# Feed-forward stages of a hybrid decoder trunk on one core: VectorE's order written out in gate and up, block sums placed tile by tile, and residual halves loaded ahead in down

## The chip, the cores and the metric

The kernel runs on one core of a Trainium2 chip. The metric is the device time of one execution in microseconds (us), as the median of several runs; less is better. The engines are TensorE (PE in the profile, PEld for its weight loads), VectorE (DVE), ScalarE (ACT), GpSimd (POOL) and SyncE (SP), which here does nothing but issue transfers (DMAs). Each engine takes its instructions in its own order and waits at an instruction until what it needs is there.

## The reference

Two layers on x of 1 x 1024 x 1024, float32. Each layer is a mix of windowed attention and a gated convolution, and then the feed-forward part, where most of this change lies:

```
h = rmsnorm(x, norm_mix); one projection h @ w_in -> q | k | v | conv value | conv gate | gate_A | gate_B
A = sliding-window attention (16 heads of 64, 2 KV heads, q and k normed, partial rotary, sinks)
B = GLU -> causal depthwise conv (width 31) -> LayerNorm -> swish -> pointwise projection
x = x + (sigmoid(gate_A) * A + sigmoid(gate_B) * B) @ w_out
h = rmsnorm(x, norm_ffn)
x = x + (silu(h @ w_gate) * (h @ w_up)) @ w_down          # D_FF = 2816 = 22 tiles of 128
```

## The kernel before, in words

All activations lie transposed: channels on partitions, the 1024 tokens along the free axis. A product of float32 matrices is made of three matmuls on parts, hi x hi, hi x lo and lo x hi. A weight is loaded raw (`fraw`, `wraw`), ACT casts its high part (`phi`, L149), and POOL or DVE subtracts that from it for the low part (`plo`, L151). `piece` does this for 512 columns. The generator `stream` yields the pieces of one layer's feed-forward in the order in which TensorE uses them; `next_p` hands out the next and keeps `PAHEAD` = 6 of them made ahead, in `NPC` = 8 buffers for each part, from 3 raw buffers.

**Gate and up.** The 22 tiles of D_FF come in the order `FORD`: 0, 11, 1, 12, and so on, so that tile p and tile p + 11 follow each other. The first two (`NCL`) are plain products. The other 20 are done as 2 x 2 block products with 7 multiplications in place of 8 (a Strassen form): gate and up are the two rows of the weight block, the two halves of the tokens the columns. Each of the 7 is 4 x 3 matmuls of 128 x 512 into a PSUM bank: `b1`, `b6`, `b7`, `b5`, `b4`, and then the products "21" and "22", which accumulate further into `b1` and `b5`. Between them DVE reads the banks: `u2` (L973), `u3` (L977), the second half of u from `b5` (L980), the first half from `b4` (L983), u times the norm factor R (L984), g's first half (L986) and second half (L988, L989). "22" can only start once L980 has read `b5`. The weight side needs sums as well: four of 512 columns for each tile (`fs`, L164).

`finish` then does silu on g (ACT, L918), g x u (POOL, L919) and the store of act (SP, L920). After the second tile of two, p + 11, it also makes the four differences of the two tiles' g that the down stage needs (DVE, L926), and stores them as `td`. Two of them overwrite the g whose store to act is under way, so they wait for it to land.

The down weights need four sums of 512 columns for each of the 11 pairs of row tiles (`dw`, L164), with two loads (L191, L192) and two stores to `sd` (L197, L198). They stand inside `stream`, so they are put into the program when the pieces ahead of them are asked for.

**Down.** Seven products again (`DOWN`: p1, p6, p2, p7, p5, p4, p3), each of 11 steps p; a step has one piece of weights and one of activations (both from memory: `wdn` or `sd`, `act` or `td`) and 4 x 3 matmuls into four banks, 132 matmuls in all. The products alternate between two sets of four banks. The last three steps (`FL` = 3) are taken together, bank by bank, so that the banks end one after the other. `evict` then reads a bank, for p2, p5, p4 and p3 into a half of the residual that `half_of` loads (L1014) at that moment (for p3 ahead of the last three steps, with `us` added, L1072); `done` writes it out and, in layer 0, makes layer 1's input from it.

**Order.** TensorE's instructions stay in the order in which the program issues them (a manual schedule). DVE's do too in a part of the in-projection; elsewhere a scheduler sets the order of DVE, ACT, POOL and SP by its own model of the times. `after(n, fn)` calls fn n ticks later; `tick()` is called at set places, as after each step of the projections, and `flush()` runs what is left.

## Time and profile before

| | us |
|---|---|
| median of 3 runs | 2760.35 (2757.0 to 2761.77) |
| the profiled execution | 2754.2 |
| its span, first to last instruction | 2752.4 |
| mean granted clock of TensorE | 0.974 |

The profile is of one execution. Durations and waits below are of that one, which is 6.15 us shorter than the median. The page's slices show three kinds of stretches: a projection, attention and convolution stretch with TensorE at 80 to 100%, then gate and up (the Strassen tiles from 756 us in layer 0 and 2121 us in layer 1) and down (1166 to 1389 us, 2534 to 2748 us). The groups of the page that belong to the feed-forward part:

```profile
L149 ACT CAST phi<-fraw 128x512 fp32r<-128x512 f32 x444 | 265.8, 620 | 500.8 <-PE b L857 344.2
L151 DVE TENSOR_TENSOR plo<-fraw,phi 128x512 fp32r<-128x512 f32 x154 | 182.4, 1191 | 143.4 <-ACT phi L149 141.4
L926 DVE TENSOR_TENSOR g<-g 128x512 f32<-128x512 f32 x88 | 119.9, 1363 | 113.2 <-DMA act<-g 63.0
```

Each line names the program line, the engine, the operation, output <- input with their shapes, the count, the busy time in us and the mean of one in ns; then the engine's idle time just before them and what ended most of it.

### The profile page before, as it was taken

The numbers are of one execution on the slowest core, as the hardware profiler recorded it, in microseconds if no ns is written. First come the engines' busy times: TensorE is split into PE (matmuls) and PEld (weight loads), VectorE is DVE, ScalarE is ACT, GpSimd is POOL, SyncE is SP. The second block draws the span as 40 slices with busy tenths as digits, with TensorE's granted clock in tenths as the row PEclk, the third lists the DMA queues.
The fourth block names the chain that finished last, engine by engine and source line by source line (L and its number), as shares of the span: only waits on it lengthen the run. The fifth ranks groups of instructions, "written<-read, shape, count | busy, mean of one in ns | idle before, by whom it ended". The sixth has DMA issues, their size and how long they took to land.

```text
span 2752.4 us, 33203 instructions
## 1 busy us (share of the span) xinstructions
PE 2596.1 (94%) x11736; PEld 2121.1 (77%) x11736; DVE 1930.6 (70%) x2053; ACT 1208.3 (44%) x2211; POOL 1598.4 (58%) x1052
## 2 busy tenths in 40 slices
PE   7998988999989999999999889899999889999998
PEld 5777777888777788878777777778887768888887
DVE  6799999551788666656737999995518777676554
ACT  2356666832522223345523666667325222323443
POOL 6477778525365666554435778775254556665544
PEclk9999999999999999999999999999999999999999
DMA  3111111475366432366721111125733654334666
GB/s 127 40 50 48 56 58 62 157 248 193 107 237 229 153 115 100 132 225 224 226 68 42 49 56 50 48 76 185 269 138 118 238 211 164 109 118 146 211 225 199
DMA packets 132358, 379.05 MB, mean 138 GB/s; under 512 B 15136, under 2 KB 15392, under 8 KB 132192
## 3 DMA queue, kind: packets, MB, share of 16 engines
q1 hardware_dynamic: 132048, 376.85, 40.1%
q8 instruction: 92, 1.51, 0.2%
q14 instruction: 74, 0.61, 0.1%
q10 hardware_dynamic: 144, 0.09, 0.0%
HBM read 259.17 MB, written 115.34 MB: 136 GB/s over the span
## 4 chain that ended last, share of the span: by engine, by line
PE 44%; DVE 15%; DMA 5%; issue 2%; ACT 2%; POOL 1%; SPq 0%; DVEq 0%; ACTq 0%; POOLq 0%
PE b L857 32%; PE ps L255 10%; DVE y L509 6%; DVE dw L164 1%; DMA dw<-wdn 1%; DVE qs L626 1%; DMA sd<-dw 1%; DVE mx L662 1%; DVE plo L151 1%; DVE sc L658 1%; ACT sc L666 1%; ACT phi L149 1%; DMA act<-g 1%; DMA fraw<-act 1%; DVE fs L164 0%
## 5 line engine op out<-in xcount | busy, mean ns | idle before, releaser
L151 POOL TENSOR_TENSOR plo<-fraw,phi 128x512 fp32r<-128x512 f32 x290 | 418.7, 1451 | 386.1 <-ACT phi L149 352.2
L149 ACT CAST phi<-fraw 128x512 fp32r<-128x512 f32 x444 | 265.8, 620 | 500.8 <-PE b L857 344.2
L509 DVE SCALAR_TENSOR_TENSOR y<-a,vec,y 128x1024 f32<-128x1024 f32 x240 | 404.8, 1687 | 4.0
L134 POOL TENSOR_TENSOR wl<-raw,wh 128x1024 fp32r<-128x1024 f32 (+1 forms) x100 | 252.0, 2522 | 230.9 <-PE ps L255 192.6
L255 PE MATMUL ps<-hx,wh 128*128 128x512 f32 x1056 | 348.8, 412 | 7.3 <-ACT hx L296 7.3
L255 PE MATMUL ps<-hx,wl 128*128 128x512 f32 x1056 | 336.3, 400 | 6.9 <-POOL wl L134 6.9
L255 PE MATMUL ps<-lx,wh 128*128 128x512 f32 x1056 | 338.2, 402 | 0.8 <-DVE lx L297 0.8
L151 POOL TENSOR_TENSOR plo<-fs,phi 128x512 fp32r<-128x512 f32 x160 | 233.2, 1473 | 117.0 <-ACT phi L149 115.0
L151 DVE TENSOR_TENSOR plo<-fraw,phi 128x512 fp32r<-128x512 f32 x154 | 182.4, 1191 | 143.4 <-ACT phi L149 141.4
L857 PE MATMUL b<-plo,phi 128*128 128x512 f32 x616 | 241.8, 393 | 10.0 <-DVE plo L151 10.0
L255 PEld LDWEIGHTS ps<-hx,wl 128*128 128x128 f32 x1056 | 204.7, 194 | 52.7 <-POOL wl L134 7.8
L255 PEld LDWEIGHTS ps<-lx,wh 128*128 128x128 f32 x1056 | 205.9, 195 | 48.4 <-DVE lx L297 2.2
L857 PE MATMUL b<-phi 128*128 128x512 f32 x616 | 240.5, 390 | 1.9 <-ACT phi L149 1.9
L857 PE MATMUL b<-phi,plo 128*128 128x512 f32 x616 | 240.5, 390 | 1.2 <-POOL plo L151 1.2
L255 PEld LDWEIGHTS ps<-hx,wh 128*128 128x128 f32 x1056 | 195.1, 197 | 42.8 <-ACT hx L296 7.3
L926 DVE TENSOR_TENSOR g<-g 128x512 f32<-128x512 f32 x88 | 119.9, 1363 | 113.2 <-DMA act<-g 63.0
L149 ACT CAST phi<-fs 128x512 fp32r<-128x512 f32 x160 | 97.7, 617 | 191.3 <-PE b L857 141.5
L919 POOL TENSOR_TENSOR g<-g,u 128x1024 f32<-128x1024 f32 x44 | 107.6, 2445 | 123.7 <-ACT g L918 84.0
L666 ACT ACTIVATE sc<-sc,nm,fq 128x129 f32<-128x129 f32 x256 | 123.7, 486 | 116.0 <-DVE nm L664 115.7
L133 ACT CAST wh<-raw 128x1024 fp32r<-128x1024 f32 (+1 forms) x100 | 98.2, 982 | 167.6 <-PE ps L255 115.8
L857 PEld LDWEIGHTS b<-plo,phi 128*128 128x128 f32 x616 | 115.9, 188 | 38.5 <-DVE plo L151 14.7
L857 PEld LDWEIGHTS b<-phi 128*128 128x128 f32 x616 | 116.0, 188 | 26.9 <-ACT phi L149 2.6
(253 smaller groups left out, 6226.0 us busy)
## 6 DMA issues: line engine op xcount, KB each, us to landing
fraw<-wgu SPq DMA_DIRECT2D x88, 512.0 KB
raw<-win SPq DMA_DIRECT2D x68, 512.0 KB
act<-g SPq DMA_DIRECT2D x44, 512.0 KB
dw<-wdn SPq DMA_DIRECT2D x44, 512.0 KB
sd<-dw SPq DMA_DIRECT2D x44, 512.0 KB
td<-g SPq DMA_DIRECT2D x44, 512.0 KB
fraw<-sd SPq DMA_DIRECT2D x88, 256.0 KB
fraw<-td SPq DMA_DIRECT2D x88, 256.0 KB
```

Source lines behind the costliest of these rows:

```text
L133: nc.scalar.copy(wh, raw)
L134: nc.gpsimd.tensor_tensor(out=wl, in0=raw, in1=wh.bitcast(F32), op=ALU.subtract)
L149: nc.scalar.copy(hi, src)
L151: (eng or nc.gpsimd).tensor_tensor(out=lo, in0=src, in1=hi.bitcast(F32), op=ALU.subtract)
L164: sub = lambda o, a, b, op=ALU.subtract: nc.vector.tensor_tensor(out=o, in0=a, in1=b, op=op)
L255: nc.tensor.matmul(ps[:, sl], a[:, wc], b[:, sl], start=first and j == 0, stop=last and j == 2)
L509: nc.vector.scalar_tensor_tensor(out=y, in0=a[:, j:j + T], scalar=V(w0 + j), in1=y, op0=ALU.mult, op1=ALU.add)
L626: after(1.5 + h, lambda hi=hi, lo=lo, h=h: nc.vector.tensor_tensor(out=qs[h][lo], in0=q32[hi], in1=qs[h][hi].bitcast(F32), op=ALU.subtract))
L666: nc.scalar.activation(sc[:, n], sc[:, n], AF.Exp, bias=nm[:, n:n + 1], scale=fq[:, 4 * j + n:4 * j + n + 1], accum_out=den[:, n:n + 1])
L857: nc.tensor.matmul(ps, w[:, ai * P:(ai + 1) * P], x, start=first and j == 0, stop=last and j == 2, skip_group_check=True)
L919: nc.gpsimd.tensor_tensor(out=g, in0=g, in1=u, op=ALU.mult)
L926: sub = lambda o, x, y: nc.vector.tensor_tensor(out=o, in0=x, in1=y, op=ALU.subtract)
```

## The change

1. **DVE's order in gate and up.** For the 20 Strassen tiles DVE gets a manual schedule as well, and the program calls `tick()` after each of the 7 products. What DVE does beside the evictions is placed by `after`.
2. **Block sums.** The sums of `dw`, their loads and stores leave `stream`. `block_sums(p, when)` makes the four of one pair at ticks 3, 4, 5, 6 of every second tile (pair 10 first, in the first Strassen tile, then pair 0, 1, and so on).
3. **finish by halves.** Silu and g x u are done for 512 columns at a time, the first half after product "21". Two of the differences of g come three ticks after the second half, the other two and the stores of `td` one tick later.
4. **Down.** Only p3 keeps its last three steps bank by bank; the others do that with the last step alone. The residual halves are loaded at steps 1 to 4 of the product that uses them (`HALVES`), and for p4 and p3 `u3` or `us` is added to them at steps 4 to 7.
5. **Buffers.** 7 piece buffers instead of 8, 5 pieces ahead instead of 6, 4 raw buffers instead of 3.
6. **Layer 1's keys and values.** The second half of K's product ends before that of V's begins; the input norm's factors are computed at once there, and the rotary step, its sum and a transpose move by one or two ticks.

```diff
-            for p in range(NG):                      # in stream()
-                if max(2 * p, NCL + 1) != i + (p == 0):
-                    continue
-                lo, up = (fq.tile([P, D], F32, tag=f"dw{k}", bufs=1, name="dw") for k in range(2))
-                nc.sync.dma_start(lo, wdn[l, p])
...
-        def finish(f, g, u):
-            nc.scalar.activation(g, g, AF.Silu)
-            nc.gpsimd.tensor_tensor(out=g, in0=g, in1=u, op=ALU.mult)
+        def finish(f, g, u, sl=slice(0, T)):
+            nc.scalar.activation(g[:, sl], g[:, sl], AF.Silu)
+            nc.gpsimd.tensor_tensor(out=g[:, sl], in0=g[:, sl], in1=u[:, sl], op=ALU.mult)
+            if sl.stop < T:
+                return
             nc.sync.dma_start(actd[f], g)
...
+            def late():
+                subs((b[:, h1], b[:, h1], a[:, h0]), (b[:, h0], b[:, h1], b[:, h0]))
+                nc.sync.dma_start(tdn[f - NG], a)
+                nc.sync.dma_start(tdn[f], b)
+            after(3, lambda: subs((a[:, h0], a[:, h1], a[:, h0]), (a[:, h1], b[:, h1], a[:, h1])))
+            after(4, late)
+
+        def block_sums(p, when):
+            lo, up = (fq.tile([P, D], F32, tag=f"dw{k}", bufs=1, name="dw") for k in range(2))
+            nc.sync.dma_start(lo, wdn[l, p])
+            nc.sync.dma_start(up, wdn[l, p + NG])
+            def last():
+                subs((up[:, h0], up[:, h0], lo[:, h0]))
+                nc.sync.dma_start(sdn[p], lo)
+                nc.sync.dma_start(sdn[p + NG], up)
+            after(when[0], lambda: nc.vector.tensor_tensor(out=up[:, h1], in0=lo[:, h1], in1=up[:, h1], op=ALU.add))
+            after(when[1], lambda: subs((lo[:, h1], lo[:, h0], lo[:, h1])))
+            after(when[2], lambda: subs((lo[:, h0], up[:, h1], lo[:, h0])))
+            after(when[3], last)
...
+        dve.enter_context(tc.manual_schedule(engines={mybir.EngineType.DVE}))
...
+            if i % 2:
+                block_sums(i // 2 - 1, (3, 4, 5, 6))
+            elif i == NCL:
+                block_sums(NG - 1, (5, 5.5, 6, 6.5))
...
             prod4(b1, next_p(), B["21"], False, True)
-            nc.vector.tensor_tensor(out=g[:, h0], in0=b1, in1=R[:, h0], op=ALU.mult)
+            add(g[:, h0], b1, R[:, h0], ALU.mult)
+            finish(f, g, u, h0)
+            tick()
...
-                x = half_of(e, 0)                    # evict, p2; p5 and p4 alike
+                x = left[e]
...
+            fl = FL if name == "p3" else 1
+            for p in range(NG - fl):
                 w, a = next_p(), next_p()
                 for e in range(4):
                     prod(bs[e], w, e, a[0], a[1], go and p == 0, False)
...
+                if 1 <= p < 5 and name in HALVES:
+                    up, n = HALVES[name]
+                    left[p - 1] = half_of(p - 1 + up, n)
+                if 4 <= p < 8 and name in ("p3", "p4"):
+                    x, u = left[p - 4], us[p - 4] if name == "p3" else u3[p - 4]
+                    nc.vector.tensor_tensor(out=x, in0=x, in1=u, op=ALU.add)
...
-        for i, (k, ns) in enumerate(kn):
-            for w, ps in ((wk, psk), (wv, psv)):
+            steps = [(k, (0, 1), both) for k in range(4, KD)] + [(k, (0,), both) for k in range(4)]
+            steps += [(k, (1,), (x,)) for x in both for k in range(4)]
...
-NPC = 8
-PAHEAD = 6
+HALVES = {"p2": (0, 0), "p5": (4, 1), "p4": (4, 0), "p3": (0, 1)}
+NPC = 7
+PAHEAD = 5
+NRAW = 4
```

What this does to the order of the engines shows in the listings below, one instruction or a run of alike ones a row. In these, `u_` with a number is u2 or u3 of a tile, `u` without one the tile's u.

DVE in gate and up of layer 0, before, in the sixth Strassen tile, one with differences of g (L926) in it:

```order
L973 TENSOR_TENSOR u_6707<-b,s 128x512
L926 TENSOR_TENSOR g<-g 128x512
L977 TENSOR_TENSOR u_6740<-b,u_6707 128x512
L926 TENSOR_TENSOR g<-g 128x512
L980 TENSOR_TENSOR u<-b,u_6740 128x512
L926 TENSOR_TENSOR g<-g 128x512
L164 TENSOR_TENSOR dw<-dw 128x512 x2
L983 TENSOR_TENSOR u<-u_6740,b 128x512
L164 TENSOR_TENSOR dw<-dw 128x512
L984 TENSOR_TENSOR u<-u,R 128x1024
```

And now, in a tile of the same kind (L978 is the helper of the evictions, L911 that of the differences):

```order
L978 TENSOR_TENSOR u_7953<-b,s 128x512
L911 TENSOR_TENSOR g<-g 128x512 x2
L164 TENSOR_TENSOR fs<-fraw,fs 128x512
L978 TENSOR_TENSOR u_7976<-b,u_7953 128x512
L911 TENSOR_TENSOR g<-g 128x512 x2
L978 TENSOR_TENSOR u<-b,u_7976 128x512
L164 TENSOR_TENSOR fs<-fraw 128x512
L164 TENSOR_TENSOR fs<-fs,fraw 128x512
L978 TENSOR_TENSOR u<-u_7976,b 128x512
L978 TENSOR_TENSOR u<-u,R 128x1024
```

The block sums have left this tile for its neighbours, and all four differences of g stand ahead of the addition into u that was L980.

SP in gate and up of layer 0, before, at the pairs 1 to 3 (`dw` loads, `sd` and `td` stores, `act` stores):

```order
L920 DMA act_1_5022<-g 128x1024
L197 DMA sd_2_5067<-dw 128x1024
L198 DMA sd_13_5078<-dw 128x1024
L191 DMA dw<-wdn 128x1024
L156 DMA fraw<-wgu 128x1024
L192 DMA dw<-wdn 128x1024
L156 DMA fraw<-wgu 128x1024
L197 DMA sd_3_5068<-dw 128x1024
L198 DMA sd_14_5079<-dw 128x1024
L191 DMA dw<-wdn 128x1024
```

And now, from the same act store's neighbours on:

```order
L928 DMA td_11_5054<-g 128x1024
L940 DMA sd_10_5075<-dw 128x1024
L941 DMA sd_21_5086<-dw 128x1024
L156 DMA fraw<-wgu 128x1024
L935 DMA dw<-wdn 128x1024
L936 DMA dw<-wdn 128x1024
L156 DMA fraw<-wgu 128x1024
L918 DMA act_1_5022<-g 128x1024
L940 DMA sd_0_5065<-dw 128x1024
L941 DMA sd_11_5076<-dw 128x1024
```

Between two act stores of a pair stood two sets of block sums' stores and loads; now pair 10's set stands ahead of them and pair 0's behind act_1, and from there on one set comes to two tiles.

DVE in layer 1's down stage, before, from the end of p4 to p3's additions of `us` to the residual half (L1072; L1035 is the eviction, `plo` the pieces' low parts):

```order
L151 TENSOR_TENSOR plo<-fraw,phi 128x512 x6
L1035 TENSOR_TENSOR x<-x,b 128x512 x3
L1072 TENSOR_TENSOR x<-x,us_20043 128x512
L151 TENSOR_TENSOR plo<-fraw,phi 128x512
L1035 TENSOR_TENSOR x<-x,b 128x512
L1072 TENSOR_TENSOR x<-x,us_20044 128x512
L151 TENSOR_TENSOR plo<-fraw,phi 128x512 x9
```

And now (L1105 adds `us`, L1066 is the eviction):

```order
L151 TENSOR_TENSOR plo<-fraw,phi 128x512 x7
L1066 TENSOR_TENSOR x<-x,b 128x512 x4
L151 TENSOR_TENSOR plo<-fraw,phi 128x512 x2
L1105 TENSOR_TENSOR x<-x,us_20122 128x512
L151 TENSOR_TENSOR plo<-fraw,phi 128x512
L1105 TENSOR_TENSOR x<-x,us_20123 128x512
L151 TENSOR_TENSOR plo<-fraw,phi 128x512 x6
```

Two of the additions of `us` stood in the midst of the evictions before; now the evictions are done together, and those two follow behind two more low parts.

More of the change, by code (lines that the diff above doesn't have):

```diff
@@ L154, in wraw @@
     def wraw(src, n=KD * P):
-        r = fw.tile([P, n], F32, tag="fraw", bufs=3, name="fraw")
+        r = fw.tile([P, n], F32, tag="fraw", bufs=NRAW, name="fraw")
         nc.sync.dma_start(r, src)
@@ L185, in stream @@
             yield piece(s4)
[L186 to L198 removed]
         for _, (a, ac), (b, bc) in DOWN:
             for p in range(NG):
[L201 removed]
+                r = fw.tile([P, D], F32, tag="fraw", bufs=NRAW, name="fraw")
                 for o, src, (row, col), w in ((c0, (wdn[l], sdn), ac, a), (c1, (actd, tdn), bc, b)):
@@ L424, in keys @@
             nc.scalar.activation(sq, ps, AF.Square)
-            rope(k32)
+            after(1 if l else NA + 0.5, lambda: rope(k32))
             f8 = sm.tile([P, 16], F32, tag="f8", name="f8")
@@ L456, in keys @@
             when_free('po', 6, norm)
-            after(7, lambda: rope_add(k32))
-            when_free('pT', 10, lambda: turn(0))
+            after(9, lambda: rope_add(k32))
+            when_free('pT', 11, lambda: turn(0))
             when_free('pT', 13, lambda: turn(1))
@@ L751, in trunk @@
         psv = psm.tile([P, 4, 2 * P], F32, tag="S", bufs=1, name="psv").rearrange("p a b -> p (a b)")
-        kn = [(k, (0, 1)) for k in range(KD)]
+        both = ((wk, psk), (wv, psv))
+        steps = [(k, (0, 1), both) for k in range(KD)]
         if l > 0:
-            kn = [(k, (0, 1)) for k in range(4, KD)] + [(k, (n,)) for n in range(2) for k in range(4)]
-        for i, (k, ns) in enumerate(kn):
-            for w, ps in ((wk, psk), (wv, psv)):
-                mm3(ps, w, slice(k * P, (k + 1) * P), xs[k], i == 0, k == kn[-1][0], ns)
-            if k < KD - 1 and (l == 0 or ns != (0,) or k % 2):
+            steps = [(k, (0, 1), both) for k in range(4, KD)] + [(k, (0,), both) for k in range(4)]
+            steps += [(k, (1,), (x,)) for x in both for k in range(4)]
+        for i, (k, ns, wps) in enumerate(steps):
+            for w, ps in wps:
+                mm3(ps, w, slice(k * P, (k + 1) * P), xs[k], i == 0, k == steps[-1][0], ns)
+            if i < 7:
                 tick()
-        after(NA, norm_a)
+        after(0 if l else NA, norm_a)
         dve = ExitStack()
@@ L915, in spread, with subs @@
                 nc.vector.tensor_tensor(out=bl, in0=t, in1=bh.bitcast(F32), op=ALU.subtract)
-        def finish(f, g, u):
-            nc.scalar.activation(g, g, AF.Silu)
-            nc.gpsimd.tensor_tensor(out=g, in0=g, in1=u, op=ALU.mult)
+        first = []
+        def subs(*ops):
+            for o, x, y in ops:
+                nc.vector.tensor_tensor(out=o, in0=x, in1=y, op=ALU.subtract)
+        def finish(f, g, u, sl=slice(0, T)):
[3 more added lines that the diff above has]
+                return
             nc.sync.dma_start(actd[f], g)
@@ L962, in half @@
             return fq.tile([P, HALF], F32, tag="c", bufs=4, name=name)
-        for f in FORD[NCL:]:
+        dve = ExitStack()
+        dve.enter_context(tc.manual_schedule(engines={mybir.EngineType.DVE}))
+        add = lambda o, x, y, op=ALU.add: nc.vector.tensor_tensor(out=o, in0=x, in1=y, op=op)
+        for i, f in enumerate(FORD):
+            if i < NCL:
+                continue
+            if i % 2:
+                block_sums(i // 2 - 1, (3, 4, 5, 6))
+            elif i == NCL:
+                block_sums(NG - 1, (5, 5.5, 6, 6.5))
             g, u = t4("g"), t4("u")
@@ L972, in trunk @@
             u2 = half("u2")
-            nc.vector.tensor_tensor(out=u2, in0=b6, in1=s, op=ALU.add)
+            add(u2, b6, s)
+            tick()
             b7 = bank()
@@ L1064, in trunk @@
             go, end = name not in ("p2", "p3"), name not in ("p1", "p5")
-            for p in range(NG - FL):
+            fl = FL if name == "p3" else 1
+            for p in range(NG - fl):
                 w, a = next_p(), next_p()
@@ L1068, in trunk @@
                     prod(bs[e], w, e, a[0], a[1], go and p == 0, False)
-            if name == "p3":
-                for e in range(4):
-                    left[e] = half_of(e, 1)
-                    nc.vector.tensor_tensor(out=left[e], in0=left[e], in1=us[e], op=ALU.add)
-            wa = [(next_p(), next_p()) for _ in range(FL)]
+                if 1 <= p < 5 and name in HALVES:
[4 more added lines that the diff above has]
+                    nc.vector.tensor_tensor(out=x, in0=x, in1=u, op=ALU.add)
+            wa = [(next_p(), next_p()) for _ in range(fl)]
             for e in range(4):
                 for i, (w, a) in enumerate(wa):
-                    prod(bs[e], w, e, a[0], a[1], False, end and i == FL - 1)
+                    prod(bs[e], w, e, a[0], a[1], False, end and i == fl - 1)
                 evict(name, e, bs[e])
```

42 lines of the change are left out of this document (16 added, 26 removed).

## The prediction

> **What bounds the kernel now.** I read the page's first part, then busy time by stretches (the two feed-forward blocks cut at their stages), then the waits of TensorE, and last the timeline around one long wait. The page first:
>
> ```profile
> PE 2596.1 (94%) x11736; PEld 2121.1 (77%) x11736; DVE 1930.6 (70%) x2053; ACT 1208.3 (44%) x2211; POOL 1598.4 (58%) x1052
> ```
>
> TensorE is busy for 94% of the span and its work is not changed, so only its gaps and its slow matmuls can be won. Which stage holds them? The next rows give, for a stretch of the span: length, busy time and instruction count of PE, PEld, DVE, ACT and POOL, granted clock, DMA share, GB/s. In order they are layer 0's first 7 Strassen tiles of gate and up and its last 13, the same for layer 1 (8 and 12), and the down stage of layer 0 and of layer 1; then three single tiles and three single down products.
>
> ```profile
> 755.90:914.90 159.00, 142.96 (x590) 114.39 (x589) 130.88 (x144) 39.66 (x64) 91.22 (x57) 0.96 0.64 232
> 914.90:1166.10 251.20, 251.20 (x1094) 205.32 (x1093) 163.17 (x182) 75.22 (x117) 152.53 (x101) 1.00 0.32 113
> 2120.90:2301.90 181.00, 164.03 (x673) 131.71 (x673) 143.85 (x156) 44.70 (x71) 105.30 (x65) 0.94 0.60 216
> 2301.90:2533.80 231.90, 231.90 (x1009) 189.53 (x1008) 158.06 (x168) 68.38 (x108) 143.98 (x93) 1.00 0.32 113
> 1166.10:1389.10 223.00, 214.23 (x925) 173.46 (x924) 140.46 (x140) 110.43 (x184) 110.28 (x76) 0.99 0.67 220
> 2533.90:2748.20 214.30, 209.98 (x925) 173.07 (x923) 116.59 (x114) 89.63 (x152) 104.36 (x74) 1.00 0.67 219
> ...
> 755.90:776.56 20.66, 19.59 (x85) 15.71 (x84) 19.92 (x22) 5.36 (x9) 15.70 (x9) 1.00 0.63 223
> 799.50:824.67 25.17, 21.94 (x85) 17.48 (x84) 19.15 (x24) 5.78 (x10) 11.91 (x8) 0.88 0.67 243
> 914.90:934.20 19.30, 19.30 (x86) 15.79 (x85) 14.18 (x18) 5.79 (x10) 11.56 (x8) 1.00 0.38 137
> 1203.34:1233.26 29.92, 29.92 (x133) 24.78 (x132) 16.24 (x15) 13.14 (x24) 15.06 (x12) 1.00 0.61 194
> 1166.09:1203.34 37.25, 32.90 (x133) 25.32 (x132) 18.35 (x15) 17.05 (x27) 20.50 (x12) 0.95 0.77 270
> 2714.95:2748.22 33.27, 30.21 (x133) 24.52 (x131) 13.96 (x16) 10.58 (x18) 13.02 (x10) 1.00 0.50 164
> ```
>
> The last 13 and 12 tiles run with PE busy throughout: 251.20 / 13 = 19.32 us a tile. That is the floor. The first 7 and 8 take 22.7 and 22.6 us each, DVE is 82% and 79% busy in them (130.88 of 159.00, 143.85 of 181.00), and the DMA share is twice that of the later tiles. The excess is 159.00 - 7 x 19.32 = 23.7 and 181.00 - 8 x 19.32 = 26.4, together 50.1 us. A down product's floor is 29.92 us; the excess there is 223.0 - 209.4 = 13.6 and 214.3 - 209.4 = 4.9, together 18.4 us. So 68.5 us is all that these two stages can give. The waits of PE for line 857 (all products) over the whole run: sum, times, longest.
>
> ```profile
> PE b L857 <- DVE u L980: 33.0, 13, 4.9
> PE b L857 <- DVE plo L151: 10.0, 10, 3.1
> PE b L857 <- POOL plo L151: 1.2, 1, 1.2
> ```
>
> L980 is the addition that reads bank b5 for the second half of u; the product "22" then accumulates into b5 and can't start before. Thirteen waits for one DVE operation make 33.0 of the 50.1. What kept it is in the timeline of the tile of 25.17 us, and of the one of 20.66:
>
> ```profile
> 773.67 0.50 PE L857 MATMUL b<-B22h,phi 128*128 128x512 f32 x1 [1.07 <-DVE u L980]
> ...
> 811.61 1.75 DVE L926 TENSOR_TENSOR g<-g 128x512 f32<-128x512 f32 x1 [1.70 <-POOL g L919]
> 811.63 0.45 SPq L920 DMA_DIRECT2D act<-g  x1
> ...
> 815.57 0.40 PE L857 MATMUL b<-B21l,phi 128*128 128x512 f32 x1
> 815.80 0.40 PE L857 MATMUL b<-B21h,plo 128*128 128x512 f32 x1
> 817.24 1.53 DVE L926 TENSOR_TENSOR g<-g 128x512 f32<-128x512 f32 x1 [3.27 <-DMA act<-g]
> 818.69 0.68 DVE L980 TENSOR_TENSOR u<-b,u 128x512 f32<-128x512 f32 x1
> 819.43 0.79 PE L857 MATMUL b<-B22h,phi 128*128 128x512 f32 x1 [3.23 <-DVE u L980]
> 820.45 0.63 PE L857 MATMUL b<-B22h,plo 128*128 128x512 f32 x1
> ```
>
> DVE stood idle for 3.27 us at a subtraction of g that may not overwrite g until the store of act, issued at 811.63, had landed; L980 stood behind it. PE waited 3.23 us, and its matmuls then begin 0.43 to 0.6 us apart instead of 0.23: the tile ran at a granted clock of 0.88 and took 5.85 us more than the floor, not 3.23. After the wait of 1.07 us the clock stayed at 1.00 and the tile took 20.66 - 19.32 = 1.34 more. So 17.1 of the 50.1 us is slow matmuls after waits.
>
> The Trainium skill, TensorE: Matmul & The Clock Gate, section "Part 1: The HAM clock gate", says that an idle window of about 3.4 us halves the array's clock and some 3.4 us of work restores it. If each of the 13 waits set it off, an estimate by that page is 13 x 1.7 = 22 us beside the 33.0, 5 more than the tiles lost, and the forecast would be 5 lower; the trace agrees in kind, but the short wait lost nothing, so I go by the tiles.
>
> **Gate and up.** DVE's work around those tiles, as groups (count, busy, mean ns, idle before); the first row from 760 to 960 us, the others but the L989 one from 960 to 1150, where there are no block sums. The L989 row, over both, gives minimum, median and maximum in ns; the L919 row is the page's, and the last, of the chain that ended last, has start and length.
>
> ```profile
> L164 DVE TENSOR_TENSOR dw<-dw 128x512 f32<-128x512 f32 x42 | 43.0, 1025 | 7.0 <-DMA dw<-wdn 6.6
> ...
> L926 DVE TENSOR_TENSOR g<-g 128x512 f32<-128x512 f32 x20 | 26.0, 1300 | 34.6 <-POOL g L919 18.0 <-DMA act<-g 16.6
> L984 DVE TENSOR_TENSOR u<-u,R 128x1024 f32<-128x1024 f32 x10 | 21.8, 2181 | 0.3
> L164 DVE TENSOR_TENSOR fs<-fraw 128x512 f32<-128x512 f32 x18 | 12.2, 680 | 0.1
> L989 DVE TENSOR_TENSOR g<-g,R x19: 677/1070/1778, 784.3 to 1147.7; 128x512 f32<-128x512 f32 x19
> L164 DVE TENSOR_TENSOR fs<-fs,fraw 128x512 f32<-128x512 f32 x9 | 10.9, 1211 | 0.0
> L980 DVE TENSOR_TENSOR u<-b,u 128x512 f32<-128x512 f32 x10 | 6.9, 685 | 0.5
> ...
> L919 POOL TENSOR_TENSOR g<-g,u 128x1024 f32<-128x1024 f32 x44 | 107.6, 2445 | 123.7 <-ACT g L918 84.0
> ...
> 1154.45 4.15 DMA act<-g
> ```
>
> Before, all 44 block sums of a layer, with their 22 loads and 22 stores, fall in the first tiles; the change gives every two tiles 4 sums, 2 loads, 2 stores. Nothing is removed. Two tiles then hold on DVE: 12 reads of PSUM x 0.685 = 8.2; u x R twice 2.18 = 4.4; 8 sums of fs, 4 at 0.68, 2 at 1.21 and 2 of a third kind taken at 0.68, = 6.5; 4 subtractions of g x 1.30 = 5.2; 4 block sums x 1.03 = 4.1; g x R twice 1.07 = 2.1. Sum 30.5 of 2 x 19.32 = 38.6 us, 79%: it fits, without much to spare.
>
> The order counts as well. Products last 19.32 / 7 = 2.76 us. In a tile with subtractions of g, from the end of product 2 (5.52) DVE now does u2, two subtractions, one fs sum, u3, two subtractions, then the addition that was L980: 3 x 0.685 + 4 x 1.30 + 0.68 to 1.21 = 7.9 to 8.5, done at 13.5 to 14.0. Product "22" starts at 6 x 2.76 = 16.56: 2.5 us to spare. With all five operations between at 1.78 it is 5.52 + 2.06 + 8.9 = 16.5, just in time. The late pair of subtractions still needs the act store. Product 7 ends the previous tile; then come g's addition and product on DVE (0.68 + 0.68 to 1.78), a silu on 512 columns and a product on POOL of half of 2.45 (the L919 row); with pieces queued ahead on ACT and POOL I estimate the issue at 4 to 5.7. It lands 4.15 (last row) to 5.6 us (811.63 to 817.24) later, at 8.2 to 11.3. DVE comes to those subtractions at about 10.5. At worst a wait of 0.8 us on DVE, inside the 2.5 spare. In a tile with block sums two of them stand there in place of four subtractions.
>
> So I take the stalls as gone, but for one mild stall of 1.34 in each layer where the first pair's block sums come with two loads back to back: 50.1 - 2.7 = **-47.4 us** (ends: -50.1, and +0 if DVE is again late as often as now).
>
> On SP the loads of dw now stand behind stores of sd, which wait for the sums; they are used 11 ticks later, some 30 us, which hides them. A fourth raw buffer and one piece buffer less leave the memory even: the streams' lead shrinks from 6 to 5 pieces. In gate and up each piece serves 12 matmuls (2.76 us), so 5 pieces are 13.8 us ahead; free.
>
> **Down.** The rows: SP's store of td and the cast that waits for a weight load at the start of layer 0's stage; then the last product of layer 1.
>
> ```profile
> 1183.72 0.32 SPq L932 DMA_DIRECT2D td<-g  x1
> ...
> 1189.71 0.62 ACT L149 CAST phi<-fraw 128x512 fp32r<-128x512 f32 x1 [7.02 <-DMA fraw<-wdn]
> ...
> 2716.53 0.33 SPq L1014 DMA_DIRECT2D x<-xs  x1
> ...
> 2719.77 0.69 DVE L1072 TENSOR_TENSOR x<-x,us 128x512 f32<-128x512 f32 x1 [5.97 <-DMA x<-xs]
> 2721.12 0.50 PE L857 MATMUL b<-plo,phi 128*128 128x512 f32 x1 [3.06 <-DVE plo L151]
> ```
>
> At layer 1's last product the residual was asked for at 2716.53 and DVE, in order, waited 5.97 us for it at 2719.77 with a piece's low part behind; PE lost 3.06, and the product took 33.27. The change loads each half in steps 1 to 4 of the same product, at least 11 - 5 steps of 29.92 / 11 = 2.72 us, so 16 us, ahead of its use: that wait goes. At the start of layer 0's stage (37.25 against 29.92) weight loads are late behind the last tiles' stores; the split of the last product into halves brings them ahead by about 1.6 us, and one more raw buffer lets a load go out a step earlier (2.72 us). That is 4.3 of 7.3. Against it: fewer piece buffers, and a product whose last step alone is done bank by bank instead of three, so the second piece of a step has 5.4 us instead of 8.2 in which to be made at the boundary with its 4 evictions. Where one is late, the row nearest in kind is POOL's late piece, 1.2 us. I keep four of those (start of layer 0's stage, three boundaries with evictions): 18.4 - 4.8 = **-13.6** (ends: -18.4; and +18.3 if 12 boundaries each lost 3.06, the longest such wait).
>
> **Layer 1's K and V heads.** PE waits for a weight's low half there:
>
> ```profile
> 1412.91 0.50 PE L255 MATMUL ps<-hx,wl 128*128 128x512 f32 x1 [0.93 <-POOL wl L134]
> ```
>
> K's second half now precedes V's, so V's weights come 12 matmuls later: **-0.9** (ends: -0.9 and 0). Rope and norm move by one or two steps beside other work: 0, bounded by that same 0.9 either way.
>
> **Sum.** -47.4 - 13.6 - 0.9 = -61.9. The profiled execution took 2754.2 (span 2752.4, 1.8 around it): 2692.3. It is 6.15 under the median of 2760.35; from the median it is **2698**. All excess gone is -68.5 - 0.9 = -69.4: 2685 from the one, 2691 from the other. The likeliest case's own range is 2685 to 2708. About 0.2%, 5.5 us, is what a measurement here tells from no change.
>
> **Rivals.**
> *Stalls stay, smaller.* The act store or a slow run of sums makes DVE 1 us late in every second tile, spread as the sums now are. For it: the window of 0.8 us above, and DVE idles 16.6 us for act stores even in the quiet tiles. Against: 2.5 us to spare. 20 tiles x 1.34 = 26.8 in place of 2.7: 2722.
>
> *The thinner lead in down.* 12 boundaries x 3.06 = 36.7 in place of 4.8: 2730. For it, TensorE already waits ten times for a low part; against, the longest of those, 3.06, stood behind a residual's load.
>
> *DVE becomes the bound (slower).* DVE's order is now fixed, so an operation slowed by POOL delays all behind it, in every tile and not in the first 15 alone. The L989 row has 0.68 alone and 1.78 at worst. If all 18 operations on SBUF operands in two tiles cost 1.78: 32.0 + 4.4 + 8.2 = 44.6 against 38.6; 20 pairs make 892 where the four stretches now make 823.1: +69 - 14.5 = 2815. It decides against the kernel from (823.1 + 14.5) / 20 = 41.9 us for two tiles, a mean of 1.63 for those 18. Against it: their mean is now 17.9 / 18 = 1.0. The Trainium skill, SBUF — State Buffer, section "SBUF: two separate sides", speaks for it: a VectorE operation with two SBUF inputs and a GpSimd one that reads SBUF take a shared port pair as an exclusive lock, and the loser waits for the whole instruction. The spread from 0.68 to 1.78 agrees; that most run at about 1.0 says that they meet for part of the time only.
>
> *It doesn't do what it says:* the sums bunch again, or the fixed order merely trades one wait for another: 2760.
>
> **Chances.** Forecast 0.70; smaller stalls 0.14; thinner lead 0.07; DVE bound 0.05; nothing 0.02; 0.02 for a gain beyond the forecast's range. The range takes the forecast and the smaller stalls: 2685 to 2724. Faster 0.93, same 0.02, slower 0.05.
>
> **What would show it.** Right: PE's wait for the addition into u under 4 us in all; the tiles from the third on at 19.3 us each, DVE near 79% in all of them, DMA even; no wait for x in the last down product and a down stage of 209 to 213 us in both layers; no drop of the granted clock in the feed-forward. Wrong: waits for u in every second tile with subtractions of g ahead on DVE (first rival); waits for low parts at product boundaries (second); tiles over 20.9 us with DVE above 95% (third).

## The result, and the profile after

The changed kernel takes 2710.95 us in the median of 4 runs (2710.9 to 2711.28), the kernel before 2758.95 us (4 runs, 2757.0 to 2761.77). The ratio is 0.9826, interval 0.9808 to 0.9843: 48.0 us or 1.7% faster. The forecast was 2698, the range 2685 to 2724; the sign is right and the time is in the range, but 14 us of the 62 did not come, and it lies 3 us above the likeliest case's own range.

First the page's first part for the changed kernel, then stretches that answer to those of before (length, then busy time and count of PE, PEld, DVE, ACT and POOL, granted clock, DMA share, GB/s): the first 8 and last 12 Strassen tiles of layer 0, the same of layer 1, the two down stages, and one tile of 21.00.

```profile
PE 2585.2 (95%) x11736; PEld 2112.5 (78%) x11736; DVE 1876.9 (69%) x2053; ACT 1196.4 (44%) x2251; POOL 1654.0 (61%) x1092
```

```profile
761.70:918.20 156.50, 155.11 (x673) 126.06 (x672) 117.34 (x129) 41.11 (x74) 107.20 (x69) 1.00 0.46 162
918.20:1151.09 232.89, 232.89 (x1010) 188.96 (x1008) 180.46 (x193) 68.64 (x124) 170.07 (x109) 1.00 0.48 166
2102.90:2261.80 158.90, 156.55 (x673) 127.31 (x672) 114.84 (x131) 41.29 (x75) 106.88 (x69) 0.99 0.45 159
2261.80:2494.55 232.75, 232.54 (x1009) 189.20 (x1008) 173.44 (x191) 68.58 (x124) 168.22 (x109) 1.00 0.48 166
1151.10:1365.80 214.70, 211.48 (x925) 172.86 (x924) 125.63 (x145) 107.99 (x186) 113.75 (x78) 1.00 0.70 235
2494.60:2705.30 210.70, 210.01 (x925) 173.02 (x923) 89.27 (x119) 88.46 (x154) 102.54 (x76) 1.00 0.68 229
...
800.30:821.30 21.00, 19.61 (x86) 15.71 (x85) 15.19 (x18) 5.59 (x10) 13.64 (x10) 1.00 0.62 226
```

DVE and the DMA share are now even (75% and 0.46 early, 77% and 0.48 late in layer 0), and the clock is 1.00 in all stretches but one. The two Strassen stretches fell from 410.2 and 412.9 us to 389.4 and 391.6, the down stages from 223.0 and 214.3 to 214.7 and 210.7. The waits of PE for line 847 (all products of the feed-forward; 857 before) and for the heads' transposes (ptk, ptv) and norm (pb) over the whole run: sum, times, longest.

```profile
PE b L847 <- DVE u L978: 3.9, 3, 2.3
PE b L847 <- DVE plo L151: 3.6, 5, 2.0
...
PE ptv L457 <- DVE kd L428: 2.9, 2, 1.5
PE ptk L424 <- DVE k L400: 2.3, 2, 1.2
...
PE pb L317 <- DVE dg L310: 1.7, 1, 1.7
```

The 33.0 us of waits for the addition into u are 3.9 now. The last three rows were not among the waits of before, and they are the way to what is missing. Cut by stages, the two profiled executions (spans 2752.4 and 2709.2) compare so:

| stretch | before, us | after, us | difference | forecast |
|---|---|---|---|---|
| layer 0 to its first Strassen tile | 755.9 | 761.7 | +5.8 | 0 |
| Strassen tiles, both layers | 410.2 + 412.9 | 389.4 + 391.6 | -42.1 | -47.4 |
| down, both layers | 223.0 + 214.4 | 214.7 + 210.8 | -11.9 | -13.6 |
| layer 1 to its first Strassen tile | 731.8 | 737.1 | +5.3 | -0.9 |

The sum is -42.9 against 43.2 between the spans. The other 5 of the 48 us lie between the profiled execution of before, 2754.2, and its median; no profile shows them.

Where the heads lose is in the timeline of layer 0, the changed kernel first: what DVE and PE do there.

```profile
62.60 1.22 DVE L451 TENSOR_TENSOR v<-psv,R 128x1024 f32<-128x1024 f32 x1
64.41 1.22 DVE L473 TENSOR_TENSOR ur<-ps,R 128x1024 f32<-128x1024 f32 x1 [0.59 <-PE ps L242]
65.55 2.55 DVE L400 TENSOR_TENSOR k<-k,rot 128x1024 f32<-128x1024 f32 x1
...
68.24 0.63 PE L424 MATMUL ptk<-ident,k 128*128 128x128 f32 x4 [1.15 <-DVE k L400]
70.34 1.09 PE L457 MATMUL ptv<-ident,v 128*128 128x128 f32 x4 [1.47 <-DVE kd L428]
...
70.00:74.00 4.00, 3.66 (x12) 3.12 (x13) 1.04 (x3) 0.74 (x2) 0.00 (x0) 0.58 0.00 0
```

The kernel before, at the same place:

```profile
63.26 1.23 DVE L413 TENSOR_TENSOR k<-k,rot 128x1024 f32<-128x1024 f32 x1
64.40 1.22 DVE L464 TENSOR_TENSOR v<-psv,R 128x1024 f32<-128x1024 f32 x1
...
70.00:74.00 4.00, 4.00 (x24) 3.35 (x24) 2.31 (x4) 0.69 (x2) 0.00 (x0) 1.00 0.09 37
```

The rotary sum k<-k,rot stood ahead of v and the conv value ur on DVE; two ticks later it stands behind both, it takes 2.55 us there instead of 1.23, and the transposes of K wait. From 70 to 74 us PE starts 12 matmuls instead of 24, at a granted clock of 0.58.

### The profile page after: what moved, and what is told of

Read it like the earlier page. It is cut to its first block, busy times and chain, and to the rows that moved or that the text cites. A ratio compares the mean times of both kernels' runs of the same rounds, so it can differ in the third digit from the quotient of the medians.

```text
span 2709.2 us, 33260 instructions
## 1 busy us (share of the span) xinstructions
PE 2585.2 (95%) x11736; PEld 2112.5 (78%) x11736; DVE 1876.9 (69%) x2053; ACT 1196.4 (44%) x2251; POOL 1654.0 (61%) x1092
## 5 line engine op out<-in xcount | busy, mean ns | idle before, releaser
L151 POOL TENSOR_TENSOR plo<-fraw,phi 128x512 fp32r<-128x512 f32 x290 | 423.0, 1467 | 229.2 <-ACT phi L149 214.7
L151 POOL TENSOR_TENSOR plo<-fs,phi 128x512 fp32r<-128x512 f32 x160 | 264.3, 1663 | 253.5 <-ACT phi L149 241.7
L149 ACT CAST phi<-fraw 128x512 fp32r<-128x512 f32 x444 | 257.6, 618 | 246.4 <-POOL plo L151 131.8
L151 DVE TENSOR_TENSOR plo<-fraw,phi 128x512 fp32r<-128x512 f32 x154 | 133.6, 873 | 187.8 <-ACT phi L149 185.5
L242 PEld LDWEIGHTS ps<-hx,wh 128*128 128x128 f32 x1056 | 195.6, 197 | 42.9 <-ACT hx L283 7.3
L915 POOL TENSOR_TENSOR g<-g,u 128x512 f32<-128x512 f32 (+1 forms) x84 | 129.4, 1558 | 31.9 <-DVE u L968 25.5
L911 DVE TENSOR_TENSOR g<-g 128x512 f32<-128x512 f32 x88 | 102.0, 1159 | 65.7 <-POOL g L915 42.5
```

What stands on the lines that cost most here:

```text
L149: nc.scalar.copy(hi, src)
L151: (eng or nc.gpsimd).tensor_tensor(out=lo, in0=src, in1=hi.bitcast(F32), op=ALU.subtract)
L242: nc.tensor.matmul(ps[:, sl], a[:, wc], b[:, sl], start=first and j == 0, stop=last and j == 2)
L911: nc.vector.tensor_tensor(out=o, in0=x, in1=y, op=ALU.subtract)
L915: nc.gpsimd.tensor_tensor(out=g[:, sl], in0=g[:, sl], in1=u[:, sl], op=ALU.mult)
```

## The experiments

**Heads undone.** Everything in the heads as before, both layers.

```diff
-            after(1 if l else NA + 0.5, lambda: rope(k32))
+            rope(k32)
-            after(9, lambda: rope_add(k32))
-            when_free('pT', 11, lambda: turn(0))
+            after(7, lambda: rope_add(k32))
+            when_free('pT', 10, lambda: turn(0))
```

(with the old loop over K's and V's steps, and `after(NA, norm_a)`)

> The changed kernel with the heads' part undone in both layers (K and V steps, input norm, rotary step, its sum and the transpose as before). Theory A: the stretch from a layer's start to its gate and up is 5.8 and 5.3 us longer after the change because the rotary sum (k<-k,rot, 1.23 us before, 2.55 after) now stands on DVE behind v and the conv value, so TensorE waits 1.15 and 1.47 us for two transposes in each layer and runs its next matmuls at a clock of 0.58. Then this kernel takes 2711 - 11 = 2700 us (2698 to 2702), with no wait over 1 us at those transposes, and layer 1's wait of 0.93 for wl is back. Rival B: the 5 us come from elsewhere (buffers and pools placed otherwise, another clock), and undoing the heads gives 2709 to 2712.

Measured: 2704.34 us (2701.8 to 2706.01), 6.6 us less than the changed kernel; no wait at ptk and ptv is left, and layer 1's wait of 0.9 for wl is back. The stretch before layer 0's tiles is 756.5 us again. Theory A holds in kind, but the gain is 4 us short of it: in the profiled run down in layer 0 took 217.2 us and layer 1's stretch 735.1, for which I have no shown cause.

**The rotary sum alone put back.** Two numbers.

```diff
-            after(9, lambda: rope_add(k32))
-            when_free('pT', 11, lambda: turn(0))
+            after(7, lambda: rope_add(k32))
+            when_free('pT', 10, lambda: turn(0))
```

> The changed kernel with two numbers put back: the rotary sum after 7 ticks instead of 9, the first transpose after 10 instead of 11; the order of K's and V's matmuls and the early norm stay as changed. Theory A, in its narrow form (the place of the rotary sum alone does it): 2700 to 2703 us, waits for the two transposes gone in both layers, the wait of 1.72 us at pb in layer 1 kept. Rival B1 (the delayed rotary step or the early norm and the K-V order carry half of it): 2704 to 2708. Rival B2: the transposes wait as long as before this edit, 2709 to 2712.

Measured: 2700.66 us (2698.65 to 2702.34), 10.3 us less than the changed kernel, as the narrow form of A has it. This kernel's DVE and clock at the place:

```profile
63.21 1.23 DVE L400 TENSOR_TENSOR k<-k,rot 128x1024 f32<-128x1024 f32 x1
64.36 1.22 DVE L451 TENSOR_TENSOR v<-psv,R 128x1024 f32<-128x1024 f32 x1
...
70.00:74.00 4.00, 4.00 (x25) 3.36 (x24) 2.31 (x4) 0.66 (x2) 0.00 (x0) 1.00 0.09 33
```

So the two ticks by which the rotary sum was moved cost 10 us in two layers. The rest of the heads' change does no harm, and by this pair of runs may be worth some 3 to 4 us; but layer 1's stretch up to its tiles, 733.9 us here and 735.1 in the run before, is longer than the 731.8 of the kernel before, so no stretch of the profiles shows where such a gain would lie.

**Gate and up alone**, in the kernel before, with its own buffers, heads and down stage.

```diff
-NPC = 7
-PAHEAD = 5
-NRAW = 4
+NPC = 8
+PAHEAD = 6
+NRAW = 3
```

(and heads and down as before)

> The kernel before with the gate and up part alone (DVE's order, block sums tile by tile, finish by halves), with its own buffers (8 pieces, 6 ahead, 3 raw), heads and down stage as before. If the stages add up: the Strassen tiles fall from 410.2 and 413.0 us to about 389.4 and 391.7, and the time is 2759 - 42 = 2717 us (2714 to 2720) with the down stage unchanged. Rival 1: the first down product's gain (37.25 to 32.91 us) comes from gate and up's end too: 2711 to 2714. Rival 2: the fourth raw buffer is needed in gate and up: 2724 or more, with waits of the kind phi <- fraw<-wgu.

Measured: 2743.75 us, ratio 0.9941 (0.9927 to 0.9955): only 15 us of the 42. The Strassen tiles took 410.4 and 406.9 us. But the stalls are not those of before: they go on to the very end of the stage. Every second tile takes 20 to 23 us, and the others are at the floor but for the second of each layer (24.6 and 23.3). That is the prediction's first rival. The stages don't add up, and the size fits the expectation that put it on the raw buffers, but its sign, waits for raw weights, isn't there: PE waits for the addition into u.

```profile
PE b L844 <- DVE u L975: 22.2, 16, 2.0
```

The lead of 6 pieces is the other difference. Two later runs tell it and the raw buffer apart. The first product of layer 0's down stage, with that stage's code as before, fell from 37.25 to 33.08 us in this kernel, as the other rival of the expectation has it.

**Down alone**, in the kernel before.

> The kernel before with the down part alone (last step alone bank by bank but for p3, residual halves loaded ahead), buffers, gate and up and heads as before. If the down stage's gain is all of this part: 2759 - 12 = 2747 us. Rival: the first product's 4.3 us belong to gate and up's end or to the fourth raw buffer, and this part only takes out the ends of p2, p5, p4 and p3: 8.3 + 3.6 - 4.3 = 7.6, so 2751 us (2750 to 2753). Should fewer steps taken bank by bank lose something without more buffers, 2755 or more, with waits for plo at product boundaries.

Measured: 2747.59 us, ratio 0.9961 (0.9947 to 0.9975), 11.5 us less than before. The two stages of this kernel:

```profile
1166.08:1381.34 215.26, 210.67 (x925) 173.12 (x924) 142.22 (x140) 109.55 (x184) 109.81 (x76) 1.00 0.69 228
2528.75:2738.20 209.45, 209.45 (x925) 173.24 (x923) 116.84 (x114) 88.57 (x152) 99.72 (x74) 1.00 0.68 224
```

223.0 and 214.4 became 215.3 and 209.5: this part alone gives all of the down gain, and with 8 piece buffers and 6 ahead layer 1 reaches the floor of 7 x 29.92 = 209.4. In layer 0 the first product took 34.8 us here; with gate and up alone it was 33.1, so each part alone shortens it and the two gains don't add up.

**Six pieces ahead**, in the changed kernel.

```diff
-PAHEAD = 5
+PAHEAD = 6
```

> The changed kernel with 6 pieces made ahead instead of 5, the buffers as changed (7 piece buffers, 4 raw). In the run of gate and up alone (6 ahead, 8 and 3 buffers) every second tile took 20.5 to 23 us. Theory P: the lead sets where the sums of fs stand in DVE's written order; with 6 ahead two of them stand ahead of the addition into u that frees bank b5, right behind the differences that wait for the act store, so the addition is 1 to 2 us late in every second tile: 20 x 1.4 = 28 us, 2738 us (2730 to 2746), waits for that addition about 25 us in all. Rival R: those stalls came from the third raw buffer that was missing, so nothing happens here: 2709 to 2714.

**Three raw buffers**, in the changed kernel.

```diff
-NRAW = 4
+NRAW = 3
```

> The changed kernel with 3 raw buffers instead of 4 and the lead as changed (5 ahead, 7 piece buffers). DVE's order in gate and up is that of the changed kernel. Theory P (the lead does it): tiles stay at 19.3 to 19.5 us and the time within 2709 to 2716, down a little longer at its start. Rival R (the fourth raw buffer does it): the stalls of the run of gate and up alone come back, 2730 to 2740.

Measured: six ahead 2740.03 us (ratio 0.9934, 0.9919 to 0.9949), 29 us more than the changed kernel; three raw buffers 2710.31 us (ratio 0.9828, 0.9812 to 0.9845), the same as with four. The lead does it. DVE with six ahead, in a tile with differences of g, and this kernel's wait row:

```profile
1063.01 1.42 DVE L911 TENSOR_TENSOR g<-g 128x512 f32<-128x512 f32 x2 [4.42 <-DMA act<-g]
1064.34 0.69 DVE L164 TENSOR_TENSOR fs<-fraw 128x512 f32<-128x512 f32 x1
1065.06 0.69 DVE L164 TENSOR_TENSOR fs<-fs,fraw 128x512 f32<-128x512 f32 x1
1065.67 0.68 DVE L978 TENSOR_TENSOR u<-b,u 128x512 f32<-128x512 f32 x1
...
PE b L847 <- DVE u L978: 20.1, 14, 2.1
PE b L847 <- ACT phi L149: 10.3, 4, 2.8
```

The sums of fs are put into DVE's order when `next_p` asks for their pieces. One piece more ahead, and two of them stand between the differences and the addition into u, 1.3 us. In the changed kernel they stand behind it. In both kernels the differences end 15.9 us into the tile (this one starts at 1048.53; the changed kernel's is shown further down), so the two sums are what is added. From the seventh tile on every second tile takes 20.7 to 21.7 us for it. The second and third tile of each layer take 23.3 to 23.9: there DVE first waits for a load of dw or for the act store, and PE's wait is put down to the high part of one of those two sums, which ACT finishes 0.1 us behind the addition. Those are the four waits of the last row. I had costed the lead at nothing ("13.8 us ahead; free") because I looked at the pieces only.

**The scheduler's order in gate and up**: no manual schedule, all else as changed.

```diff
-        dve = ExitStack()
-        dve.enter_context(tc.manual_schedule(engines={mybir.EngineType.DVE}))
...
-        dve.close()
```

> The changed kernel without the manual schedule of DVE in gate and up: the block sums still come to every second tile by ticks, finish stays in halves, but the scheduler orders DVE. If the bunching of the block sums alone made the stalls: Strassen tiles of 19.3 to 19.6 us and 2706 to 2716 us. If the written order is needed as well (the scheduler puts sums and differences ahead of the addition into u again): waits for that addition in most tiles, 2725 us or more.

Measured: 2754.25 us, ratio 0.9987 (0.9978 to 0.9997). Nearly nothing is left but the down gain, set off by the heads' loss. The first 7 tiles, the other 13, and DVE's groups of block sums in the first 7:

```profile
763.35:924.10 160.75, 141.90 (x587) 113.66 (x586) 133.28 (x140) 39.45 (x68) 96.98 (x64) 0.95 0.63 227
924.10:1176.40 252.30, 252.30 (x1096) 205.99 (x1096) 160.63 (x182) 78.51 (x132) 151.29 (x115) 1.00 0.34 118
```

```profile
L911 DVE TENSOR_TENSOR dw<-dw 128x512 f32<-128x512 f32 x30 | 37.6, 1253 | 0.3
L942 DVE TENSOR_TENSOR dw<-dw 128x512 f32<-128x512 f32 x11 | 11.1, 1009 | 9.9 <-DMA dw<-wdn 9.7
```

(The cut lies 1 us ahead of the seventh tile's end.) 41 of the layer's 44 sums are back in the first 7 tiles: the ticks set only the order in which the program issues, and the scheduler, by what the rows show, takes an operation as soon as it can. So this run doesn't tell bunching and order apart; it shows that without a written order there is no spreading. The next one does tell.

**Block sums at one place**, DVE's order written: the four sums of a pair back in `stream`.

> The changed kernel with the block sums put back into the stream of pieces, DVE's order as the program writes it: the four sums of a pair then stand in one place, in the tiles that also have the four differences of g, ahead of the addition into u. If DVE's sum ahead of that addition decides, as the prediction reckons it: 5.5 + 7.9 to 8.5 + 4 x 1.03 = 17.5 to 18.1 us, plus the wait for the act store, against 16.56 at which the product starts, so 1 to 3 us late in every second tile, 20 x 2 = 40: about 2750 us (2730 to 2775). Rival: DVE has room enough in a tile wherever the sums stand, 2711 to 2718.

Measured: 2728.86 us, ratio 0.9891 (0.9876 to 0.9906): 18 us more than the changed kernel, less than half of what I had reckoned, and outside both expectations. From the seventh tile on every second tile takes 20.34 us.

```profile
PE b L860 <- DVE u L991: 17.8, 16, 3.4
```

The written order (with finish in halves and the lead of 5), with one lump of four sums in every second tile, gives more than half of the gain (the Strassen tiles take 398.8 and 398.7 us instead of 410.2 and 412.9); taking the lump apart gives the rest, 9.4 and 7.1 us. The sums cost less than the 1.03 us that I took: 0.689 in this kernel's quiet tiles.

**Residual halves loaded late**: `half_of` at the evictions, for p3 ahead of its last three steps, as before; all else as changed.

```diff
-                x = left[e]
+                x = half_of(e, 0)                    # p2; p5 and p4 alike, with u3 added there
```

> The changed kernel with the residual halves loaded where they are used, at the evictions (for p3 ahead of its last three steps, with us added there), all else as changed. If the loads ahead are what shortened p4 and p3 (32.33 and 32.97 to 30.92 and 30.86 us in layer 0, 31.49 and 33.28 to 29.91 and 30.87 in layer 1): 1.4 + 2.1 + 1.6 + 2.4 = 7.5 us come back, 2718 us (2716 to 2722), with PE waiting for plo behind DVE's wait for x. Rival: taking only the last step bank by bank did it, and the loads are hidden anyway: 2709 to 2713.

**Three steps last in every product.**

```diff
-            fl = FL if name == "p3" else 1
+            fl = FL
```

> The changed kernel with the last three steps of every down product taken bank by bank, as before, with 7 piece buffers. Theory: the three steps hold 6 of the 7 buffers until the last bank is through, so the next product's second piece can't be begun, and each of 12 boundaries loses 0.5 to 1.5 us: 2717 to 2729 us, waits for plo at the boundaries 6 us or more. Rival (the one of the prediction: the thin last step costs at p5, p4 and p3, 0.4 + 1.0 + 0.9 us in layer 0 and about the same in layer 1, and three steps would take that out): 2706 to 2709.

Measured: late halves 2710.29 us (ratio 0.9823, 0.9807 to 0.9839), no loss. Three steps last 2730.9 us (ratio 0.9896, 0.9881 to 0.991), 20 us more, with the halves loaded ahead; p4 and p3 take 34.94 and 34.96 us in layer 1, 33.9 and 35.3 in layer 0. My theory of the boundaries was wrong as well: most products lose nothing (29.95 to 30.07). For layer 1 the loss is in DVE's order at the end of p4, with the PE wait behind it:

```profile
2685.72 0.69 DVE L1066 TENSOR_TENSOR x<-x,b 128x512 f32<-128x512 f32 x1 [1.35 <-PE b L847]
2688.64 0.69 DVE L1105 TENSOR_TENSOR x<-x,us 128x512 f32<-128x512 f32 x1 [2.23 <-DMA x<-xs]
2689.25 1.75 DVE L151 TENSOR_TENSOR plo<-fraw,phi 128x512 fp32r<-128x512 f32 x1
2690.92 0.68 DVE L1066 TENSOR_TENSOR x<-x,b 128x512 f32<-128x512 f32 x1
...
2691.05 0.80 PE L847 MATMUL b<-plo,phi 128*128 128x512 f32 x1 [3.10 <-DVE plo L151]
```

It is the picture of before (5.97 and 3.06 us there). With three steps bank by bank the evictions come 2.04 us apart, and the scheduler puts the addition of us, which waits for a load, between the third and the fourth, ahead of the pieces' low parts. With one step they come together, 4 in 2.5 us, and that addition goes behind the low parts. Not the early load, but the short last step took the stall out there. Not all of the 20 us is this step's: the kernel before, with three steps too but 8 piece buffers and 6 pieces ahead, had down stages of 223.0 and 214.4 us, against 224.5 and 219.8 here.

Nor did the load ahead take DVE's wait for the residual away. In the changed kernel:

```profile
DVE x L1105 <- DMA x<-xs: 10.7, 4, 5.4
```

The longest of the four, 5.36 us, is in the last down product of all, as the 5.97 was. DVE stood at the addition of us from 2678.54, the load of that half was issued at 2678.66 only, and DVE went on at 2683.90. But p4's four evictions and two more low parts were done before that wait, and PE lost 0.6 us to a late low part in the whole stage of layer 1.

**The rotary sum back, and the late pair of differences a tick later.** The rows of the changed kernel that led there, from a tile in its middle (DVE, then POOL and SP; the tile starts at 1034.67):

```profile
1044.92 0.69 DVE L911 TENSOR_TENSOR g<-g 128x512 f32<-128x512 f32 x1 [2.43 <-POOL g L915]
1047.64 2.90 DVE L911 TENSOR_TENSOR g<-g 128x512 f32<-128x512 f32 x2 [0.83 <-DMA act<-g]
1050.46 0.68 DVE L978 TENSOR_TENSOR u<-b,u 128x512 f32<-128x512 f32 x1
...
1039.40 2.53 POOL L151 TENSOR_TENSOR plo<-fraw,phi 128x512 fp32r<-128x512 f32 x2
1041.90 2.98 POOL L915 TENSOR_TENSOR g<-g,u 128x512 f32<-128x512 f32 x2
...
1044.91 0.33 SPq L918 DMA_DIRECT2D act<-g  x1
```

POOL makes four low parts ahead of g x u, so act is stored 10.2 us into the tile (I had estimated 4 to 5.7), and the addition into u is done at 16.5, with "22" due at 16.56. There is no margin; in layer 0 every second tile from the fifth on takes some 19.48 us, in layer 1 only a few take more than the floor.

```diff
-            after(4, late)
+            after(5, late)
```

> The changed kernel with the rotary sum and the transpose back at 7 and 10 ticks (2700.7 us by itself), and the second pair of differences of g a tick later, behind the addition into u that frees bank b5. If that pair's wait for the act store is what is left of the stalls in gate and up (20.95 and 23.0 us tiles, and 19.48 in every second tile): the tiles come to 19.32 but for the one that waits for POOL; the 40 tiles fall from 779.4 us (with the rotary sum back) to 773 to 776, and the time to 2694 to 2698. Rival: the rest is DVE's waiting for POOL's product and the delayed pair only moves it on to u x R and g: 2699 to 2703.

Measured: 2695.59 us (2693.77 to 2697.93), ratio 0.9769 (0.9755 to 0.9784), 5.1 us less than with the rotary sum alone. The 40 tiles take 387.7 + 387.0 = 774.7 us (779.4 before this edit), and from the fifth tile on all are at 19.32 or 19.33.

**The lead by stage**: that kernel, with 6 pieces ahead in down and 5 in gate and up.

```diff
-        ahead(PAHEAD)
+        ahead(PAHEAD + lead[0])          # lead[0] = 1 while down runs
```

> The kernel of the run before this one, with 6 pieces ahead in the down stage and 5 in gate and up. With 6 ahead throughout, down took 212.9 and 209.8 us against 214.7 and 210.8 of the changed kernel (the first product 30.14 against 32.91). If that lead is what helped there: 2 to 3 us less than the run before, 2691 to 2695. Rival: the short first product came from the stalls in gate and up, which gave the loads time, and the lead does nothing: within 1 us of the run before.

Measured: 2691.59 us (2689.96 to 2695.16), ratio to the kernel before 0.9756 (0.9742 to 0.9771), the best of all. Its Strassen tiles and down stages, layer 0 and then layer 1:

```profile
755.03:1141.56 386.53, 386.53 (x1682) 315.73 (x1681) 292.36 (x324) 110.83 (x199) 274.73 (x179) 1.00 0.47 166
1141.56:1355.58 214.02, 211.53 (x925) 172.86 (x924) 123.79 (x142) 107.88 (x185) 111.07 (x78) 1.00 0.71 235
2088.73:2475.95 387.22, 387.01 (x1681) 315.56 (x1680) 290.46 (x324) 110.86 (x199) 273.66 (x179) 1.00 0.48 166
2475.95:2685.78 209.83, 209.76 (x925) 173.14 (x923) 88.50 (x116) 87.70 (x153) 101.21 (x76) 1.00 0.68 229
```

The tiles stand at the floor of 20 x 19.32 = 386.4 and 0.8 above, down at 214.0 and 209.8 (216.0 and 210.8 in the run before). The 4 us between the medians are a little more than the 2.9 us of the two down stages. The ranges of the two runs overlap by 1.4 us, so the size is only roughly known. The first product of layer 0 took 32.1 us, not the 30.15 of six ahead throughout, so most of what was short there came with the stalls in gate and up, as the rival has it.

## Why the prediction was right or wrong

**Gate and up: right in size, and closer to failing than it said.** -42.1 of -47.4. That DVE's lateness at one addition held nearly all, and that the clock's loss goes with the waits, is shown: 33.0 us of waits became 3.9, and the clock of the early tiles rose from 0.96 and 0.94 to 1.00 and 0.99. The term that was mis-sized is the rest: a mild stall in each layer kept at 1.34, which was 1.6 and 3.7 us, and 0.16 us in many of the other second tiles. The step behind it is the time of the act store, 10.2 us into the tile, not 4 to 5.7; the pieces queued ahead on POOL were named but put too small, since four low parts stand there. The margin of 2.5 us was nearly 0. The store then landed within 2.7 us and not 5.6, which saved it. That is luck as far as the prediction goes.

**The lead of 5: a step costed at nothing that carries 29 us.** The run with six ahead is the first rival, as it was described, in nearly every second tile. The prediction named the rival but not its switch.

**The heads: the step that failed.** "Rope and norm move by one or two steps beside other work: 0, bounded by that same 0.9 either way." It cost 10 us (2710.95 to 2700.66 with two numbers put back). The bound was taken from the wait that was there and not from what would stand ahead on DVE; the order of DVE in the head, v and ur ahead of k<-k,rot, could have been read before. Without this step the kernel stands 3 us from the forecast. The other term, -0.9 for K and V, can't be told: the wait of 0.93 for wl is gone, a wait of 1.7 at pb has come in layer 1 (1.2 with the heads as before), and the stretch scatters by more than that from run to run.

**Down: right size, wrong mechanism.** -11.9 of -13.6. "The change loads each half ... that wait goes": it did not go (5.36 us against 5.97). The load was issued when DVE already stood at the addition of us, not 16 us ahead, and with the loads at the old place nothing is lost (2710.29). The thin last step, entered as a cost of three boundaries, is what brings the gain at the end of p4 in layer 1: with three steps the stages take 224.5 and 219.8 us. What stays is p5 to p3 at 30.3 to 30.9 us and the start of layer 0's stage: 5.3 + 1.3, against the 4.8 that were kept. The difference is a slip in the sum: by the prediction's own reckoning 7.3 - 4.3 = 3.0 us stay at that start, and it entered 1.2; measured were 32.91 - 29.92 = 3.0. That the 4.3 came out is luck in part. The first product fell nearly as far with gate and up alone and 3 raw buffers (33.08). With 3 raw buffers in the changed kernel it took 35.4 in the profiled execution, but with 4 it was 32.9 to 34.6, at the same lead of 5. So no run shows the 2.72 us of a raw buffer, and the cause of that gain stays open.

**The rivals.** DVE did not become the bound: 72 to 77% busy in the four stretches, a little under the 79% reckoned, and two tiles take 38.8 us, far from 41.9. The rotary sum took 1.23 us where POOL did nothing beside it. Where it took 2.55, from 65.55 to 68.10 us, POOL's low part of a weight had begun at 64.61 and ended at 67.02, 1.08 ahead of the sum's end; in layer 1 the sum, 2.54 us long, ends 1.07 behind the POOL operation. That agrees with the Trainium skill's rule of the shared port pair (SBUF — State Buffer, "SBUF: two separate sides"), by which the later of the two waits for the whole of the other. No run here takes the POOL operation away, so it is not shown as the cause.

**The signs.** Of those named as right, the waits for u under 4 us (3.9) and the even DMA share came. The tiles at 19.3 from the third on (20.95 and 23.0 there), DVE near 79% (72 to 77%), no wait for x in the last product (5.36) and 209 to 213 us for both down stages (214.7 and 210.7) did not come in full. The one drop of the clock left is 0.99 in layer 1's first tiles.

## What to carry to other kernels

An operation's cost on an in-order engine is its place: ask for each step that is moved, by however few ticks, and for each count that sets how early something is issued (a lead, a number of buffers), what then stands ahead of the one operation for which the bound engine waits. Where a scheduler orders an engine, as here, spreading work in the program's text may spread nothing; the written order did. And bunch the evictions of a product's banks where a scheduler fills their gaps with operations that may wait for a load.

## What the runs showed of the hardware that was not expected

Short waits slowed TensorE in the heads as well: two waits of 1.15 and 1.47 us, 2 us apart, were followed by 4 us at a granted clock of 0.58 (in single microseconds from 69 to 74: 0.97, 0.50, 0.50, 0.50, 0.82), so that 2.6 us of waiting cost some 5 (10.3 us in the medians, for two layers; 5.6 in layer 0's stretch). A single wait of 1.07 us in gate and up left the clock at 1.00. The Trainium skill (TensorE: Matmul & The Clock Gate, "Part 1: The HAM clock gate") ties the drop to an idle window of about 3.4 us; here PE was idle for 2.3 of 4 us, in two pieces, as the row shows, and that was enough.

```profile
66.00:70.00 4.00, 1.72 (x9) 0.98 (x7) 3.19 (x3) 0.00 (x0) 1.02 (x1) 0.99 0.41 131
```

One act store of the same 512 KB landed in 2.7 us in the changed kernel (issued at 1044.91, the difference behind it starting at 1047.64), where the last load had been issued 4.2 us before it. It took 6.0 us with six pieces ahead (1056.97 to 1063.01), where a load of raw weights was issued 3.6 us and one of dw 0.4 us before it. That those loads are the cause is not shown.
